# Cosine-similarity attention on one core: SyncE holds back the loads of the third pair until K of the first pair has landed

## The chip, the cores and the metric

The kernel runs on one core of a Trainium2 chip. Five engines work side by side, each through an instruction queue of its own, in order: TensorE (PE; its weight loads are listed as PEld), VectorE (DVE), ScalarE (ACT), GpSimd (POOL) and SyncE (SP), which here does nothing but issue transfers. ScalarE issues three transfers itself. The transfers are carried out by 16 DMA engines; SyncE and ScalarE each feed a queue of their own (q1 and q10 in the profile). An engine waits for another, or for a transfer, on a semaphore; a transfer has landed when its semaphore has counted 16, one from each DMA engine. The metric is the device time of one execution in microseconds, and smaller is better.

## The reference

For each of 8 batches and 12 heads, Q, K and V have 512 rows of 64 float32 numbers. Rows of Q and K are scaled to length 1, their scores are divided by tau = 0.1, and a softmax weights the rows of V:

```python
Q_norm = Q / (np.linalg.norm(Q, axis=-1, keepdims=True) + 1e-10)
K_norm = K / (np.linalg.norm(K, axis=-1, keepdims=True) + 1e-10)
scores = np.einsum('bhqd,bhkd->bhqk', Q_norm, K_norm) / tau
weights = np.exp(scores - np.max(scores, axis=-1, keepdims=True))
weights = weights / (np.sum(weights, axis=-1, keepdims=True) + 1e-10)
return np.einsum('bhqk,bhkd->bhqd', weights, V).astype(np.float32)
```

## The kernel before, in words

**Pairs.** Heads are worked on two at a time: 96 heads make 48 pairs, numbered from s = 0 in the code; the text counts from the first, so the third pair is s = 2. For a pair, Q, K and V are loaded in one transfer each of 256 KB (lines 310 to 314); a tile row of 128 partitions holds four rows of each head. The first pair is the exception: Q and K come in halves of one head, 128 KB each, Q on SyncE's queue and K on ScalarE's (lines 304 to 309).

**What happens to a pair.** Its Q and K are squared (in most pairs on GpSimd, L337; in the second pair on ScalarE with half of K on GpSimd, and in the third Q on ScalarE, L329, and K on GpSimd, L331). The squares are summed, partly on TensorE (L354) with a reduction on VectorE (L361). From the sums come the inverse lengths: for the first four pairs by a logarithm and an exponential on ScalarE (L248 and L252 for the first pair, L379 and L382 for the next three), later by steps on VectorE. Q and K are scaled with them (L258, L420), transposed on TensorE (L266, L268, L426) and copied back (L279, L434). TensorE then makes the scores, 512 x 512 a head, in four blocks (L508); ScalarE takes exp of each block, both heads in one instruction (L531; in the first pair's first two blocks one head at a time); TensorE multiplies with V (L548), which GpSimd has converted (L536); VectorE divides (L559, L561) and SyncE stores (L565).

**Order.** Operations are recorded with the operations that they need (`needs`), and each becomes one or several instructions. The order on each engine is a list written out by hand, `ORDER` (line 644), of the operations' numbers. `write` (line 69) turns an operation's needs into waits on semaphores just ahead of its instruction, so a wait stops everything behind it on that engine. SyncE's list begins

```python
"sp": (
    "7 8 64 65 103 104 11 141 142 66 179 180 105 222 223 143 ..."
```

which is: 7 and 8 the two halves of the first pair's Q; 64 and 65 Q and K of the second pair; 103 and 104 Q and K of the third; 11 V of the first; 141 and 142 Q and K of the fourth; 66 V of the second; 179 and 180 Q and K of the fifth; 105 V of the third; and so on. Stores come into the list after 33 loads. The halves of the first pair's K are 9 and 10, the first two entries of ScalarE's list.

ScalarE's list begins

```python
"act": (
    "9 10 3 12 25 16 18 17 29 31 67 30 68 106 44 74 75 40 41 45 112 47 113 ..."
```

where 3 loads the function table, 12 and 25 square the first pair's Q, 16 to 31 are the first pair's inverse lengths, 67 squares Q of the second pair, 30 is the last inverse length of the first pair, 68 squares half of K of the second pair, 106 squares Q of the third pair, and 44 is the first exponential of scores; 74 and 75 are the inverse lengths of the second pair, 112 and 113 those of the third.

**Buffers.** There are 15 buffers for Q and K of a pair and 10 for V (`RINGS`), so the first loads wait for no buffer: without the change, none of the transfers in the list's beginning waits for anything.

**Names.** `("LD", s, w)` is the load of Q (w = 0) or K (w = 1) of pair s, `("LD", 0, w, h)` that of head h of the first pair, `("LV", s)` that of V; `qk` is the buffer of Q and K, `sq` the squares, `qn` the scaled rows, `qt` the transposed ones, `scps` the scores, `et` their exponentials.

Of the kernel before, what the change touches and what calls it, by code (L numbers as in the profile page):

```python
# [108 lines left out]
def bass_cosine_similarity_attention_kernel(  # L109
# [15 lines left out]
    R_QK, R_V, R_SQ, R_QN, R_QT, R_ET, R_O, R_X = RINGS  # L125
# [31 lines left out]
    P = Program(nc)  # L157
# [15 lines left out]
    def src(x, s):  # L173
        b, h = divmod(2 * s, NHEAD)
        return x[b, h : h + 2].rearrange("h (p t) d -> p h (t d)", t=NT)

    def key(name, s, *rest):
        return (name, s) + rest if s >= 0 else None
# [111 lines left out]
    def squares(s, w):  # L290
        return [("SQ", s, w if s in SQ_ON else 0)] + ([("SQ", s, w, 1)] if s in SQ_ON and isinstance(SQ_ON[s][w], tuple) else [])
# [5 lines left out]
    def pair(s):  # L297
# [6 lines left out]
        for w, x in ((0, Q), (1, K)):  # L304
            if s == 0:
                for h in range(2):
                    P.add(("LD", 0, w, h), "act" if w else "sp", "ldh", -1000 + h,  [],
                          lambda e, w=w, x=x, h=h: e.dma_start(out=qk[iq][:, w, h], in_=src(x, s)[:, h]), slot=f"head{w}_{h}")  # L308
                continue
            P.add(("LD", s, w), "sp", "ld1" if s == 1 else "ld", s, [*([("SCL", 0, w, 0), ("SCL", 0, w, 1), ("SQ", 0, w, 0), ("SQ", 0, w, 1)] if s == R_QK else [key("SCL", s - R_QK, w), *(squares(s - R_QK, w) if s >= R_QK else [])])],  # L310
                  lambda e, w=w, x=x: e.dma_start(out=qk[iq][:, w], in_=src(x, s)),  # L311
                  slot=f"first{s}_{w}" if s <= 3 else f"qk{iq}")
        P.add(("LV", s), "sp", "ld", s + VLAG, [key("VC", s - R_V)],
# [32 lines left out]
        for w in range(2):  # L346
# [16 lines left out]
            else:  # L363
                P.add(("RED", s, w), "dve", "red", due_red(s) + 0.5 * w, [*sqs, ("NRMS", 0, 0, 1), *new(g - R_X), *last_direct(s)],
                      lambda e, w=w, dst=dst: e.tensor_reduce(  # L365
                          out=dst, in_=sq[iqs][:, 8 * w : 8 * w + 8, :], axis=AX.X, op=ALU.add))
# [47 lines left out]
        for w in range(2):  # L414
# [5 lines left out]
                  lambda e, w=w, r=r: e.tensor_tensor(  # L420
                      out=qn[iqn][:, w].rearrange("p t h d -> p h t d"),
                      in0=qk[iq][:, w].rearrange("p h (t d) -> p h t d", t=NT), in1=r, op=ALU.mult))
# [174 lines left out]
    for s in range(NP):  # L597
        pair(s)
# [171 lines left out]
```

## Time and profile before

| What | Value |
|---|---|
| time before, median of 3 runs (lowest, highest) | 189.58 us (189.12, 190.11) |
| the profiled execution's own time | 189.78 us |
| its span, first to last instruction | 187.8 us |
| ScalarE busy | 180.4 us, 96% of the span |
| TensorE busy | 173.9 us, 93% |
| VectorE busy | 173.0 us, 92% |
| GpSimd busy | 166.7 us, 89% |
| TensorE's clock, granted | 0.995 |
| bytes moved | 50.76 MB, 270 GB/s in the mean |

The groups of instructions that matter here (line, engine, operation, tiles, count; busy us, mean ns of one; idle time before them and what ended it):

```profile
L531 ACT ACTIVATE et<-scps 128x1024 bf16<-128x1024 f32 (+1 forms) x191 | 174.1, 1170 | 0.0
...
L331 POOL TENSOR_TENSOR sq<-qk 128x512 bf16<-128x512 f32 (+1 forms) x4 | 3.7, 932 | 2.0 <-DMA qk<-in_K_dram 2.0
```

ScalarE's exponentials alone take 174.1 us of the 187.8. Its other work and its idle time lie in the first 16 us and in the last two or three. The page's rows of transfers give, for each kind of issue, how long it took from issue to landing, in the median:

```profile
vf<-in_V_dram SPq DMA_DIRECT2D x48, 256.0 KB, 6.0
qk<-in_Q_dram SPq DMA_DIRECT2D x47, 256.0 KB, 5.3
qk<-in_K_dram SPq DMA_DIRECT2D x47, 256.0 KB, 6.1
...
qk<-in_Q_dram SPq DMA_DIRECT2D x2, 128.0 KB, 2.6
qk<-in_K_dram ACTq DMA_DIRECT2D x2, 128.0 KB, 2.8
```

and the rate over the span in 40 slices of 4.7 us, where the first three slices are the part of the kernel that the change touches:

```profile
DMA  5999999899999998999999799995987722311333
GB/s 162 326 355 350 348 354 330 258 316 320 380 384 379 349 332 250 336 276 337 378 382 366 220 285 379 362 328 162 317 294 226 244 85 71 112 58 62 110 108 121
```

An issue (DMA_DIRECT2D on SPq or ACTq) is the time in which the engine hands a transfer over; the transfer itself follows. On the timeline, rows of SPq are issues, not transfers.

### The profile page before, as it was taken

To read this page: it belongs to the slowest core of one execution; us is meant where nothing else is said; L and a number is where in the kernel's file an instruction comes from. 1 tells how busy PE (TensorE), PEld (TensorE's weight loads), DVE (VectorE), ACT (ScalarE), POOL (GpSimd) and SP (SyncE) were. 2 spreads that over 40 slices of the span, in tenths; PEclk is the share of its full clock that TensorE was granted. 3 is DMA by queue.
4 is the path that set the end of the run, shared out by engine and by line. 5 is a ranking of instruction groups with operands and counts; after the bars stand their busy time and mean duration, and the time that the engine had idled before them with its cause. 6 is when DMAs were issued, how large, how long until landed. Compare 5 with 4: busy or idle time off the path is not lost.

```text
span 187.8 us, 6632 instructions
## 1 busy us (share of the span) xinstructions
PE 173.9 (93%) x2694; PEld 108.4 (58%) x2694; DVE 173.0 (92%) x546; ACT 180.4 (96%) x212; POOL 166.7 (89%) x152
## 2 busy tenths in 40 slices
PE   6799899999998999999999999999999889999993
PEld 2455566566565666666566666556655556655562
DVE  2688999999999999999999999999999999998873
ACT  4699999999999999999999999999999999999992
POOL 5499999999999999999999999999999999965600
PEclk9999999999999999999999999999999999999998
DMA  5999999899999998999999799995987722311333
GB/s 162 326 355 350 348 354 330 258 316 320 380 384 379 349 332 250 336 276 337 378 382 366 220 285 379 362 328 162 317 294 226 244 85 71 112 58 62 110 108 121
DMA packets 52446, 50.76 MB, mean 270 GB/s; under 512 B 3136, under 2 KB 52416, under 8 KB 52416
## 3 DMA queue, kind: packets, MB, share of 16 engines
q1 hardware_dynamic: 51984, 50.02, 80.7%
q8 instruction: 21, 0.34, 0.8%
q10 hardware_dynamic: 432, 0.33, 0.5%
q14 instruction: 9, 0.07, 0.1%
HBM read 37.75 MB, written 12.58 MB: 268 GB/s over the span
## 4 chain that ended last, share of the span: by engine, by line
ACT 93%; DMA 3%; SPq 1%; issue 1%; PE 1%; DVE 1%
ACT et L531 92%; DMA qk<-in_Q_dram 3%; PE ops L576 1%; SPq L311 0%; SPq L308 0%; DVE ob L589 0%; ACT sq L329 0%; ACT ys L379 0%; ACT nps L382 0%; DVE rd L587 0%; PE tps L576 0%
## 5 line engine op out<-in xcount | busy, mean ns | idle before, releaser
L531 ACT ACTIVATE et<-scps 128x1024 bf16<-128x1024 f32 (+1 forms) x191 | 174.1, 1170 | 0.0
L337 POOL TENSOR_TENSOR sq<-qk 128x1024 bf16<-128x1024 f32 x44 | 82.7, 1893 | 0.5 <-DMA qk<-in_K_dram 0.5
L508 PE MATMUL scps<-qt 64*128 64x512 bf16 x380 | 75.2, 386 | 7.3 <-ACT et L531 3.5
L548 PE MATMUL ops<-vb,et 128*128 128x65 bf16 x1504 | 73.4, 194 | 0.1
L548 PEld LDWEIGHTS ops<-vb,et 128*128 128x128 bf16 x1504 | 55.7, 98 | 28.7 <-issue 21.1
L561 DVE TENSOR_TENSOR ob<-ops,rd 128x256 f32<-128x256 f32 x94 | 38.7, 418 | 0.4
L420 DVE TENSOR_TENSOR qn<-qk,nps 128x512 bf16<-128x512 f32 x58 | 38.6, 676 | 0.5 <-ACT nps L382 0.5
L420 POOL TENSOR_TENSOR qn<-qk,rk 128x512 bf16<-128x512 f32 x36 | 37.5, 1054 | 1.0 <-DVE rk L394 0.9
L426 PE MATMUL tps<-ident,qn 128*128 128x128 bf16 x376 | 33.9, 221 | 0.4 <-POOL qn L420 0.2
L434 DVE COPY qt<-tps 128x1024 bf16<-128x1024 bf16 x47 | 32.2, 684 | 1.3 <-PE tps L426 0.9
L508 PEld LDWEIGHTS scps<-qt 64*128 64x128 bf16 x380 | 18.8, 92 | 24.9 <-ACT et L531 11.7
L365 DVE TENSOR_REDUCE nps<-sq 128x8 f32<-128x512 bf16 x48 | 32.5, 681 | 0.0
L536 POOL TENSOR_SCALAR vb<-vf 128x512 bf16<-128x512 f32 x48 | 30.3, 646 | 0.2
L426 PEld LDWEIGHTS tps<-ident,qn 128*128 128x128 bf16 x376 | 21.5, 98 | 12.8 <-issue 6.0
L354 PE MATMUL ops<-sq,ident 128*128 128x64 bf16 x368 | 18.4, 193 | 0.8 <-ACT nps L252 0.8
L559 DVE RECIPROCAL rd<-ops 128x4 f32<-128x4 f32 x94 | 16.1, 175 | 2.9 <-PE ops L548 2.2
L354 PEld LDWEIGHTS ops<-sq,ident 128*128 128x128 bf16 x368 | 13.7, 98 | 3.9 <-issue 2.0
L361 DVE TENSOR_REDUCE nps<-ops 128x8 f32<-128x64 f32 x40 | 8.7, 217 | 0.6 <-PE ops L354 0.4
L480 POOL TENSOR_TENSOR xz<-xz 128x1024 f32<-128x1024 f32 x2 | 3.8, 1892 | 3.3 <-DVE xz L475 3.3
L389 DVE TENSOR_TENSOR nps<-nps,ys 128x32 f32<-128x32 f32 (+1 forms) x30 | 6.2, 208 | 0.2
L390 DVE SCALAR_TENSOR_TENSOR nps<-nps,ys 128x32 f32<-128x32 f32 (+1 forms) x30 | 6.2, 208 | 0.0
L331 POOL TENSOR_TENSOR sq<-qk 128x512 bf16<-128x512 f32 (+1 forms) x4 | 3.7, 932 | 2.0 <-DMA qk<-in_K_dram 2.0
(61 smaller groups left out, 64.2 us busy)
## 6 DMA issues: line engine op xcount, KB each, us to landing
vf<-in_V_dram SPq DMA_DIRECT2D x48, 256.0 KB, 6.0
qk<-in_Q_dram SPq DMA_DIRECT2D x47, 256.0 KB, 5.3
qk<-in_K_dram SPq DMA_DIRECT2D x47, 256.0 KB, 6.1
out_dram<-ob SPq DMA_DIRECT2D x47, 256.0 KB, 4.2
qk<-in_Q_dram SPq DMA_DIRECT2D x2, 128.0 KB, 2.6
qk<-in_K_dram ACTq DMA_DIRECT2D x2, 128.0 KB, 2.8
out_dram<-ob SPq DMA_DIRECT2D x1, 128.0 KB, 1.7
out_dram<-ob ACTq DMA_DIRECT2D x1, 64.0 KB, 1.6
```

What stands on the lines that cost most here:

```text
L337: lambda e: e.tensor_tensor(out=sqf, in0=data, in1=data, op=ALU.mult))
L354: last = e.matmul(out=o_ps[bank][:, 320:384], lhsT=ident[:, :], rhs=sq[iqs][:, 8 * w : 8 * w + 8, 8 * k : 8 * k + 8], start=(k == 0), stop ...
L365: lambda e, w=w, dst=dst: e.tensor_reduce(out=dst, in_=sq[iqs][:, 8 * w : 8 * w + 8, :], axis=AX.X, op=ALU.add))
L420: lambda e, w=w, r=r: e.tensor_tensor(out=qn[iqn][:, w].rearrange("p t h d -> p h t d"), in0=qk[iq][:, w].rearrange("p h (t d) -> p h t d" ...
L426: last = e.transpose(t_ps[:, w, t, :], qn[iqn][:, w, t].rearrange("p h d -> p (h d)"), ident[:, :])
L434: lambda e: e.tensor_copy(out=qt[iqt][:, :, :, :].rearrange("p w t x -> p (w t x)"), in_=t_ps[:, :, :, :].rearrange("p w t x -> p (w t x)")))
L508: last = e.matmul(out=sc_ps[:, 2 * b + h, :], lhsT=qt[iqt][64 * h : 64 * h + 64, 1, c, :], rhs=qt[iqt][64 * h : 64 * h + 64, 0, :, :], sta ...
L531: lambda e, c=c, b=b, hs=hs: e.activation(out=et[iet][:, c, hs[0] : hs[-1] + 1, :], in_=sc_ps[:, 2 * b + hs[0] : 2 * b + hs[-1] + 1, :], f ...
L536: lambda e: e.tensor_scalar(out=vb[:, iq, :, :, 0:DIM].rearrange("p c h d -> p h c d"), in0=vf[iv][:, :, :].rearrange("p h (c d) -> p h c ...
L548: last = e.matmul(out=o_ps[h][:, 65 * t : 65 * t + 65], lhsT=et[iet][:, c, h, 128 * t : 128 * t + 128], rhs=vb[:, iq, c, h, :], start=(c = ...
L559: lambda e, h=h, grid=grid: e.reciprocal(out=rd[io][:, h, :], in_=grid[:, :, DIM]))
L561: lambda e, h=h, grid=grid: e.tensor_tensor(out=ob[io][:, h], in0=grid[:, :, 0:DIM], in1=rd[io][:, h, :].unsqueeze(2).to_broadcast([128, N ...
```

## The change

The load of Q of the third pair, `("LD", 2, 0)`, gets one more need: `("LD", 0, 1, 1)`, the load of K of the first pair's second head. SyncE thus waits on that load's semaphore (16 counts) before it issues operation 103, and all that stands behind 103 in its list waits with it. The lists of all engines are unchanged, and so are all other needs.

```diff
-            P.add(("LD", s, w), "sp", "ld1" if s == 1 else "ld", s, [*([("SCL", 0, w, 0), ("SCL", 0, w, 1), ("SQ", 0, w, 0), ("SQ", 0, w, 1)] if s == R_QK else [key("SCL", s - R_QK, w), *(squares(s - R_QK, w) if s >= R_QK else [])])],
+            P.add(("LD", s, w), "sp", "ld1" if s == 1 else "ld", s, [*([("LD", 0, 1, 1)] if (s, w) == (2, 0) else []), *([("SCL", 0, w, 0), ("SCL", 0, w, 1), ("SQ", 0, w, 0), ("SQ", 0, w, 1)] if s == R_QK else [key("SCL", s - R_QK, w), *(squares(s - R_QK, w) if s >= R_QK else [])])],
                   lambda e, w=w, x=x: e.dma_start(out=qk[iq][:, w], in_=src(x, s)),
                   slot=f"first{s}_{w}" if s <= 3 else f"qk{iq}")
```

## The prediction

> **What bounds the kernel now.** I began with the page's chain of work that ended last, then had the same chain in order of time, and then the timelines of ScalarE and SyncE over the first 16 us.
>
> ```profile
> ## 4 chain that ended last, share of the span: by engine, by line
> ACT 93%; DMA 3%; SPq 1%; issue 1%; PE 1%; DVE 1%
> ```
>
> ```profile
> 2.67 5.60 DMA qk<-in_Q_dram
> 8.27 0.02 issue
> 8.29 0.63 ACT sq L329
> 8.92 0.48 ACT et L531
> ...
> 15.53 167.90 ACT et L531 x183
> ```
>
> The reader is to see two regimes. From 8.29 us on, ScalarE works without a gap to 183.43 us, so the end follows from when that run begins. What releases its beginning is a transfer: Q of the third pair, issued at 2.67 us and landed 5.60 us later, and that is the first load that the change holds back. ScalarE's own lines say where it stood still before:
>
> ```profile
> 5.64 0.20 ACT L252 ACTIVATE xs<-ys 128x4 f32<-128x4 f32 x1
> 6.85 0.63 ACT L329 ACTIVATE sq<-qk 128x512 bf16<-128x512 f32 x1 [1.01 <-DMA qk<-in_Q_dram]
> 7.39 0.16 ACT L252 ACTIVATE nps<-ys 128x4 f32<-128x4 f32 x1
> 7.61 0.42 ACT L329 ACTIVATE sq<-qk 128x256 bf16<-128x256 f32 x1
> 8.29 0.63 ACT L329 ACTIVATE sq<-qk 128x512 bf16<-128x512 f32 x1 [0.27 <-DMA qk<-in_Q_dram]
> 8.83 0.58 ACT L531 ACTIVATE et<-scps 128x512 bf16<-128x512 f32 x1
> ```
>
> Each row is start, duration, instruction and, in brackets, the idle time before it. It waits 1.01 us for Q of the second pair and 0.27 us for Q of the third; its queue is in order, so the first exponential (L531) stands behind both squares. A later landing of the third pair's Q therefore moves the end one for one, and an earlier one can return at most these 1.28 us.
>
> **The change, part by part.** It adds one wait in SyncE's queue and nothing else: no instruction, transfer or position in any queue changes. SyncE comes to the gated load at 2.67:
>
> ```profile
> 2.16 0.47 SPq L311 DMA_DIRECT2D qk<-in_K_dram  x1
> 2.67 0.47 SPq L311 DMA_DIRECT2D qk<-in_Q_dram  x1
> 3.18 0.47 SPq L311 DMA_DIRECT2D qk<-in_K_dram  x1
> 3.70 0.47 SPq L314 DMA_DIRECT2D vf<-in_V_dram  x1
> 4.21 0.56 SPq L311 DMA_DIRECT2D qk<-in_Q_dram  x1
> ```
>
> *When the gate opens.* K of the first pair goes out on ScalarE's queue in two halves, the two issues together 0.79 to 1.68 us. For the second the issue view says 2.9 us to landing, and GpSimd, which squares both halves in 0.612 us each without a gap from 3.56, takes it at 4.17. So the gate opens at about 4.15 and the third pair's Q is issued at 4.2 instead of 2.67: 1.5 us later. Behind it, in SyncE's order, stand K of the third pair, V of the first, Q and K of the fourth, V of the second and so on; all move by 1.5 us at first.
>
> *What hides it.* A load issued into this queue is not short of time, it stands in line. The third pair's Q took 5.6 us to land in the trace, but SyncE's queue at 33.44 us, nearly drained, shows the same 256 KB load without a line before it:
>
> ```profile
> 33.44 0.47 SPq L311 DMA_DIRECT2D qk<-in_Q_dram  x1
> ...
> DMA to landing us min/median/max: 2.8/2.8/2.8
> ```
>
> So 4.2 + 2.8 = 7.0 us is the earliest landing after the change. The line before it is unchanged: K of the second pair is issued at 2.16 as before and lands 5.4 us later, at 7.6; from there on the loads landed 0.7 us apart (issue plus landing: 7.6, 8.3, 9.0, 9.8, 10.5, 11.3, 12.0). Whoever is queued by the time its predecessor ends lands one step behind it: 7.6 + 0.7 = 8.3, as before. Cost of the gate on this load: 0. If the cover goes, because the second pair lands sooner, the bound is 7.0, which is 1.3 us before the 8.27 of the trace; so the K that opens the gate could land 1.2 us later than it did and still cost nothing.
>
> *The loads behind it.* The same restart gives their landings when the line is short: 36.2, 37.0, 38.1, 39.1, 39.8, 41.1 and 41.8, that is 0.93 us apart in the mean against 0.74 in the long line. Put on 4.2 us that is 7.0, 7.7, 8.8, 9.9, 10.6 and 11.9, each before the 8.3, 9.0, 9.8, 10.5, 11.3 and 12.0 of now. The bound from the bad side takes both: the old 8.3 for the first and 0.93 for each step, which gives 9.2, 10.1, 11.0, 11.9, so 0.2 us late for K of the third pair up to 0.6 for K of the fourth. Their slack:
>
> ```profile
> 9.10 1.04 POOL L331 TENSOR_TENSOR sq<-qk 128x512 bf16<-128x512 f32 x1 [0.84 <-DMA qk<-in_K_dram]
> ...
> 10.68 0.23 DVE L361 TENSOR_REDUCE xs<-ops 128x8 f32<-128x64 f32 x1
> ...
> 11.19 0.32 ACT L379 ACTIVATE ys<-xs,eps 128x16 f32<-128x16 f32 x1
> ```
>
> K of the third pair goes through GpSimd's square, TensorE and a reduction that ends at 10.91, and ScalarE's logarithm wants it at 11.19: 0.28 us of slack, so 0.2 is free. K of the fourth is squared as the second of two that GpSimd does from 10.81 (2.04 us together), so it is wanted at about 11.83 and would come 0.1 late; the logarithm at 14.20 has its input at 14.14. That makes 0 to 0.1 us on ScalarE. I take 0, the nearer side, since the line is still there when the gate opens. SyncE itself catches up: it issues in 0.5 us steps what the transfers take 0.7 for, and from 10.65 us on the old queue held it back at about 0.7 per issue anyway.
>
> *What could be gained.* The gate keeps SyncE quiet from 2.63 to 4.2 us. The stretches there (PE, weight loads, DVE, ACT, POOL, clock, DMA share, GB/s) show that transfers were slow just then:
>
> ```profile
> 3.20:4.20 1.00, 1.00 (x4) 0.37 (x3) 0.42 (x1) 0.61 (x2) 0.61 (x1) 1.00 0.92 243
> 4.20:5.20 1.00, 1.00 (x5) 0.45 (x4) 1.00 (x3) 0.73 (x4) 0.61 (x1) 1.00 0.69 210
> ```
>
> From 2.0 to 3.2 us it was 321 GB/s. If the issuing behind them caused the dip, it cost (321 - 243) + (321 - 210) = 189 KB, or 0.59 us of landing for the second pair. Bounds: 0 to 0.59, and 1.28 if all of ScalarE's waiting went. I take 0, because the same slowness (267 to 312 GB/s a microsecond from 34 to 39 us) stands at the other place where the line is short, with SyncE issuing at the same 0.47 us pace as here; a gate makes the line shorter, not longer.
>
> Does the gate speed K itself? In the stretch 2.0 to 4.2 us the issue view gives 0.37 MB to SyncE's queue and 0.26 MB to ScalarE's, so the two do share; but K's halves land 2.7 and 2.9 us after issue and Q's 2.5 and 2.8. Bound: 0.2 us at most.
>
> The Trainium skill, DMA: Bandwidth & Descriptors, section on queues, rings and completion order, has each engine consume one row's descriptors in ring order and take turns between rows. By that rule the third pair's packets stand behind the second pair's on SyncE's row, and holding them back frees nothing for K or for the second pair: the sum would be 0 and the faster rival falls. By the row of the dip alone it would be up to -0.59 us. The trace agrees in that SyncE's loads land in the order of issue.
>
> **Sum.** Gate on the third pair's Q 0, loads behind it 0 (to +0.1), gain for the second pair 0 (to -0.59): 0.0. Against the profiled execution that is 189.78 us (span 187.8 and 2.0 around it), which lies 0.2 above the median of the runs shown, 189.58. On the median I forecast 189.6, with the forecast's own range 189.1 to 190.1, the spread of those runs.
>
> **The rivals.**
>
> *Slower: the line is not what sets the landing.* If issue to landing stays at 5.6 us for the third pair's Q (every load from 1.69 to 4.81 us took 5.1 to 6.5), it lands at 4.2 + 5.6 = 9.8, ScalarE waits 1.5 us more at the square L329 and every exponential behind it moves: 191.1. It decides from the point where that landing passes 8.27. Against it: the 2.8 us at 33.44, and 3.0 and 3.6 for the two behind. For it: the second pair's line may hide a slow stretch of transfers that comes with any restart, and the third pair would now meet it, in the one place with no slack. Chance 0.27.
>
> *Faster: the issuing caused the dip.* Then the second pair's Q lands 0.59 to 1.0 us sooner and the wait before L329 shrinks; TensorE's sums, the head's second half and the first exponential follow. 0.6 to 1.28 us off: 188.3 to 189.0, middle 188.6. For it: the dip's place, right behind four issues without a pause. Against it: the dip at 34 to 39 us. Chance 0.22.
>
> *The gate does nothing*, K having landed by the time SyncE comes: excluded by 1.5 us in this execution; it would be 189.6. Chance 0.02; forecast 0.49.
>
> **How the numbers follow.** Half a per cent (0.95 us) is about what a measurement of this kernel can tell from no change. Forecast and idle gate lie within it (0.51), the slower rival beyond it (0.27), the faster around its edge and counted beyond it (0.22). The range reaches to both: from 188.5, which leaves out only the full 1.28, to 191.1.
>
> **What would show it.** In the changed trace SyncE's third pair goes out at 4.2; right, if its landing takes about 4.1 us instead of 5.6 and ScalarE's square of it still starts near 8.3, with the exponentials gapless behind. The slower rival shows as a wait well over 0.27 us there, the faster as a wait under 1.01 before the second pair's square and over 243 and 210 GB/s in the two stretches. A gap in ScalarE after 11 us would refute the slack of the loads behind; a first pair's K that lands after 5.4 us would refute the gate's time.

## The result, and the profile after

| | Before | After |
|---|---|---|
| median of 22 runs each | 189.28 us | 189.84 us |
| lowest, highest | 188.90, 190.11 | 189.22, 190.90 |
| the profiled execution's own time, its span | 189.78, 187.8 us | 189.81, 187.9 us |

The ratio after to before is 1.0034, with a 95% interval of 1.0018 to 1.005: 0.34% slower, some 0.6 us, inside the half per cent that the prediction called no change, but clear of 1. It is the only set of runs of the changed kernel: the experiments below were timed in three later sets on three chips, each beside runs of the kernel before, and in these the changed kernel ran only singly.

Part of the difference is in a few executions. In five of the 22 changed runs TensorE's granted clock was 0.991 over the span; these are the five slowest, 190.57 to 190.90 us. The other 17, at 0.995 and above, have a median of 189.81, so the median does not hang on them. Of the kernel before, no run that the comparisons in three other sets use, 64 in all, is under 0.995.

The two profiled executions differ by 0.1 us of span only: the one of before had a late beginning among its kind, as further traces show below. What the change does can be read from them all the same. First the chain of waits of the changed kernel in order of time (start, length, what):

```profile
1.23 3.16 DMA qk<-in_K_dram
4.38 0.02 issue
4.40 3.98 DMA qk<-in_Q_dram
8.38 0.02 issue
8.40 0.63 ACT sq L329
...
15.65 167.89 ACT et L531 x183
```

The chain now begins with K of the first pair on ScalarE's queue, which lands at 4.38 and opens the gate; the third pair's Q is issued at 4.40 and lands 3.98 us later at 8.38, where it took 5.60 us from 2.67 to 8.27 before. The same end, by another way. ScalarE's timeline in the changed kernel (start, length, instruction, idle time before it):

```profile
5.88 0.20 ACT L252 ACTIVATE xs<-ys 128x4 f32<-128x4 f32 x1
6.00 0.61 ACT L329 ACTIVATE sq<-qk 128x512 bf16<-128x512 f32 x1
6.52 0.16 ACT L252 ACTIVATE nps<-ys 128x4 f32<-128x4 f32 x1
6.61 0.40 ACT L329 ACTIVATE sq<-qk 128x256 bf16<-128x256 f32 x1
8.40 0.63 ACT L329 ACTIVATE sq<-qk 128x512 bf16<-128x512 f32 x1 [1.39 <-DMA qk<-in_Q_dram]
8.94 0.58 ACT L531 ACTIVATE et<-scps 128x512 bf16<-128x512 f32 x1
```

The wait of 1.01 us for the second pair's Q is gone: the data landed at 5.88, 0.95 us sooner than in the first trace of the kernel before. All of it went into the wait for the third pair's Q, 1.39 us in place of 0.27. A gain and a new wait of nearly the same size, behind each other on one in-order queue. The stretches (PE, weight loads, DVE, ACT, POOL, clock, DMA share, GB/s) show both sides on the DMA engines:

```profile
3.20:4.20 1.00, 1.00 (x4) 0.36 (x3) 0.42 (x1) 0.51 (x2) 0.61 (x1) 1.00 0.77 240
4.20:5.20 1.00, 1.00 (x4) 0.44 (x3) 0.86 (x3) 0.81 (x4) 0.61 (x1) 1.00 0.84 282
5.20:6.20 1.00, 0.88 (x8) 0.39 (x6) 0.64 (x2) 0.69 (x5) 0.65 (x2) 1.00 0.64 196
```

From 4.2 to 5.2 us the transfers run at 282 GB/s instead of 210, while the second pair comes in; from 5.2 to 6.2 they fall to 196, where before it was 299. Further traces bear both out: 282 to 336 GB/s in the first of these stretches in three traces of the changed kernel against 210 to 262 in four of the kernel before, and 196 to 237 in the second against 299 to 345. That reads as a line running dry while what SyncE issued at 4.40 is not flowing yet; it is worked out from the rates, and the counts below support it.

### The profile page after: what moved, and what is told of

It is laid out like the page before. It is cut to its first block, busy times and chain, and to the rows that moved or that the text cites. A ratio compares the mean times of both kernels' runs of the same rounds, so it can differ in the third digit from the quotient of the medians.

```text
span 187.9 us, 6632 instructions
## 1 busy us (share of the span) xinstructions
PE 174.4 (93%) x2694; PEld 108.7 (58%) x2694; DVE 172.9 (92%) x546; ACT 180.3 (96%) x212; POOL 166.8 (89%) x152
## 4 chain that ended last, share of the span: by engine, by line
ACT 93%; DMA 4%; PE 1%; issue 1%; DVE 1%; ACTq 0%
ACT et L531 92%; DMA qk<-in_Q_dram 2%; DMA qk<-in_K_dram 2%; PE ops L576 1%; DVE ob L589 0%; ACT sq L329 0%; ACT ys L379 0%; ACT nps L382 0%; ACTq L308 0%; DVE rd L587 0%; PE tps L576 0%
```

## The experiments

One table holds the reading of all traces, so that single landings are not made too much of; the recorded expectations call a profiled execution a look. "Lands" is the time at which the load's semaphore has its sixteenth count in the trace; "step" is how long the third pair's Q lands behind the second pair's K; "exp" is the start of the first exponential of scores.

| Trace | third pair's Q issued | second pair's Q lands | second pair's K | third pair's Q | step | exp | span |
|---|---|---|---|---|---|---|---|
| before | 2.67 | 6.83 | 7.58 | 8.27 | 0.69 | 8.83 | 187.8 |
| before, e5 | 2.67 | 6.15 | 6.86 | 7.53 | 0.67 | 8.09 | 187.1 |
| before, e6 | 2.67 | 6.75 | 7.43 | 8.17 | 0.74 | 8.73 | 187.7 |
| before, e11 | 2.68 | 6.50 | 7.25 | 7.98 | 0.73 | 8.54 | 187.5 |
| changed | 4.40 | 5.88 | 6.52 | 8.38 | 1.86 | 8.94 | 187.9 |
| changed, e7 | 4.17 | 5.57 | 6.25 | 7.66 | 1.41 | 8.22 | 187.3 |
| changed, e12 | 4.05 | 5.51 | 6.18 | 7.86 | 1.68 | 8.42 | 187.4 |
| changed, exp first, e4 | 4.07 | 5.51 | 6.19 | 8.22 | 2.03 | 8.04 | 187.6 |
| gate earlier, e9 | 3.37 | 5.51 | 6.14 | 8.03 | 1.89 | 8.59 | 187.6 |
| gate later, e3 | 6.03 | 6.01 | 6.69 | 8.73 | 2.04 | 9.29 | 189.3 |
| gate one load down, e2 | 2.67 | 6.11 | 6.79 | 7.48 | 0.69 | 8.04 | 187.1 |
| gate two down, e1 | 2.67 | 5.44 | 6.43 | 7.15 | 0.72 | 7.71 | 186.9 |
| gate two down, later, e10 | 2.67 | 6.15 | 6.88 | 7.55 | 0.67 | 8.11 | 187.6 |
| before, exp first, e8 | 2.67 | 5.29 | 6.49 | 7.16 | 0.67 | 8.07 | 187.6 |

In every trace in which the third pair's Q goes out ungated, it lands 0.67 to 0.74 us behind the second pair's K (8 of 8); in every one in which a gate stands ahead of it, 1.41 to 2.04 us behind (6 of 6). And in all traces of the kernel before and of the changed one the span is 179.0 to 179.1 us more than the start of the first exponential, of which the last 4.4 us lie behind the last exponential.

A load lands with the last of its sixteen counts, one from each DMA engine, and the traces hold each count. They show that the longer step has two parts. The eighth count of the third pair's Q comes 1.12 to 1.42 us behind the eighth of the second pair's K in the changed kernel (e4 included), against 0.68 to 0.89 in the eight ungated traces: the whole load is late. On top of that a few engines lag in some traces: in e4 fifteen counts are in at 7.05 and the sixteenth at 8.22. In e9 the eighth count is only 0.94 behind and fifteen are in at 7.24, but the sixteenth comes at 8.03. The second pair's Q has such stragglers too: eight of its counts are in at 4.64 to 5.09 us in all fourteen traces, and the last few counts spread its landing from 5.29 to 6.83.

### Gate two loads down (e1)

V of the first pair and all behind it wait; Q and K of the third pair do not.

```diff
-        P.add(("LV", s), "sp", "ld", s + VLAG, [key("VC", s - R_V)],
+        P.add(("LV", s), "sp", "ld", s + VLAG, [key("VC", s - R_V), *([("LD", 0, 1, 1)] if s == 0 else [])],
```

> The gate is moved two loads down: Q and K of the third pair go out as before the change (2.67 and 3.18 us), and V of the first pair and all behind it wait for K of the first pair's second head. Theory T (trade): the change has two effects that cancel: with SyncE quiet, Q of the second pair lands about 0.9 us sooner (5.9 against 6.8), and Q of the third pair, issued late, lands no sooner than before (8.4). Then here, with fewer issues behind the second pair than before the change, Q of the second pair lands at 6.0 to 6.5, Q of the third at 7.0 to 7.7, ScalarE's wait ahead of the third pair's square stays under 0.5 us, and the time is 0.4 to 0.9 us below the kernel before (ratio 0.995 to 0.998). Rival S (scatter): the second pair's sooner landing in the changed kernel's trace was chance; then Q of the second pair lands at 6.5 to 7.0, Q of the third at 8.0 to 8.4, and the time is that of before within 0.3 us.

Measured: 189.12 us against 189.18, ratio 0.9998 (0.9979 to 1.0017). ScalarE in its trace:

```profile
5.72 0.61 ACT L329 ACTIVATE sq<-qk 128x512 bf16<-128x512 f32 x1
...
7.17 0.63 ACT L329 ACTIVATE sq<-qk 128x512 bf16<-128x512 f32 x1 [0.30 <-DMA qk<-in_Q_dram]
7.71 0.58 ACT L531 ACTIVATE et<-scps 128x512 bf16<-128x512 f32 x1
```

Both waits are short and the exponentials begin 1.1 us before those of the first trace of the kernel before, as theory T said, with the second pair's Q even sooner (5.44) than its 6.0 to 6.5; but the median does not follow (theory S). The profiled execution, at 188.90 us, was below its own median. So no cost shows once the third pair's Q and K are ahead of the gate; a gain does not show.

### Gate one load down (e2)

```diff
-[*([("LD", 0, 1, 1)] if (s, w) == (2, 0) else []), ...
+[*([("LD", 0, 1, 1)] if (s, w) == (2, 1) else []), ...
```

> The gate is moved one load down: Q of the third pair goes out at 2.67 us as before the change, K of the third pair and all behind it wait for K of the first pair's second head. Theory T: Q of the second pair lands at 5.9 to 6.3, Q of the third right behind the second pair's K, at 6.8 to 7.4, so ScalarE's two waits both shrink; K of the third pair is issued at 4.4 and lands at 8.2 to 8.6, no later than before (9.03). Time 0.5 to 1.2 us below the kernel before (ratio 0.994 to 0.997). Rival S: second pair's Q at 6.5 to 7.0, third pair's Q at 8.0 to 8.4; K of the third pair comes late; the time is 0 to 0.5 us above the kernel before.

Measured: 189.28 us against 189.18, ratio 0.9997 (0.9979 to 1.0014). Only the third pair's Q has been taken out of the gate, everything behind it is still held (its K is issued at 4.26), and no cost shows: this interval ends below the one in which the changed kernel's ratio lies (1.0018 to 1.005). So the median's cost hangs on this one load being behind the gate, as far as different sets can be compared; the changed kernel was not run beside e1 and e2. K of the third pair, held by over a microsecond, lands at 8.15 all the same, sooner than in any trace of the kernel before (8.25 to 9.03). The gain that theory T wanted did not come here either.

### Gate later (e3)

```diff
-[*([("LD", 0, 1, 1)] if (s, w) == (2, 0) else []), ...
+[*([("LD", 1, 0)] if (s, w) == (2, 0) else []), ...
```

> The gate waits for Q of the second pair instead of K of the first: it opens at about 5.9 us, 1.5 us later than in the change. If the third pair's Q sets the start of the gapless run and its landing follows its own issue (theory T, 4.0 us from issue to landing in the changed kernel), it lands at 9.3 to 9.9, ScalarE waits 1.0 to 1.5 us longer ahead of its square, and the time is 1.5 to 2.0 us above the kernel before (ratio 1.008 to 1.011). If its landing is set by the line before it, as predicted (rival L), or by 2.8 us from issue on an empty line, it lands at 8.3 to 8.7 and the time stays within 0.3 us of the changed kernel (ratio 1.002 to 1.005).

Measured: 191.16 us against 189.18, ratio 1.0105 (1.0066 to 1.0144). The time is theory T's, but the landing is the rival's: the third pair's Q landed 2.7 us after its issue, at 8.73, where T had 9.3 to 9.9 and 2.8 us on an empty line gives 8.3 to 8.7. So T met the time by luck. The gate is so late that the line is empty, and the stretches of this kernel show what a restart costs when nothing hides it (columns as above):

```profile
6.50:7.00 0.50, 0.47 (x10) 0.28 (x10) 0.50 (x3) 0.50 (x3) 0.34 (x2) 1.00 0.00 0
7.00:7.25 0.25, 0.25 (x10) 0.23 (x6) 0.25 (x2) 0.13 (x1) 0.25 (x1) 1.00 0.58 98
7.25:7.50 0.25, 0.25 (x4) 0.09 (x1) 0.22 (x2) 0.00 (x0) 0.12 (x1) 1.00 0.72 119
7.50:8.00 0.50, 0.50 (x11) 0.34 (x11) 0.47 (x2) 0.00 (x0) 0.00 (x0) 1.00 0.92 307
```

Issued at 6.03, the load moves no byte until 7.0 and the rate is 307 GB/s from 7.5. The first exponential is 0.35 us later than in the changed kernel's first trace, and the span 1.4 us longer. The rest came behind. ScalarE's timeline shows two gaps, both ended by scores from TensorE:

```profile
14.10 1.02 ACT L531 ACTIVATE et<-scps 128x1024 bf16<-128x1024 f32 x1 [0.17 <-PE scps L508]
15.61 1.02 ACT L531 ACTIVATE et<-scps 128x1024 bf16<-128x1024 f32 x1 [0.29 <-PE scps L508]
```

TensorE's granted clock (the third number from the end) fell to half just there. These are the same stretch of e3 and of the changed kernel:

```profile
12.17:15.58 3.41, 3.37 (x31) 1.63 (x29) 2.27 (x5) 2.98 (x5) 2.67 (x4) 0.50 1.05 351
```

```profile
12.17:15.58 3.41, 3.25 (x52) 2.01 (x50) 2.78 (x6) 3.41 (x8) 3.12 (x3) 1.00 1.09 362
```

TensorE was busy all through it in e3, with 31 matmuls instead of 52, and a pair of score matmuls took 0.61 us instead of 0.39. That explains the gaps of this one execution. It does not explain the set: four of its six runs have a clock of 0.995 to 0.998 and still take 190.67 to 191.23 us. What delays those was not traced; in e10 below, loads that come late make such a gap at full clock. The changed kernel's trace has no gap between 10 and 42 us.

### The changed kernel with the first exponential ahead of the square (e4), and the same exchange before the change (e8)

```diff
-"9 10 3 12 25 16 18 17 29 31 67 30 68 106 44 74 75 ..."
+"9 10 3 12 25 16 18 17 29 31 67 30 68 44 106 74 75 ..."
```

> The changed kernel with one exchange in ScalarE's list: the first exponential of scores stands ahead of the third pair's square instead of behind it. If ScalarE's in-order wait for the third pair's Q is what the change costs (theory T), 0.4 to 0.6 us of that wait (1.39 us) is filled with the exponential, and the time falls by 0.4 to 0.6 us from the changed kernel, to about that of the kernel before (ratio 0.999 to 1.001). If the cost lies elsewhere, in K of the third pair or the loads behind (rival B), TensorE's sums of the third pair and the logarithm stay late, and the time stays at that of the changed kernel (ratio 1.003 to 1.004).

Measured: 189.54 us against 189.18, ratio 1.0017 (0.9998 to 1.0036), between theory T's range and rival B's.

> The kernel before with the first exponential ahead of the third pair's square in ScalarE's list. If the third pair's Q sets the start of the gapless run in most executions of the kernel before too, and not in its first look alone, then up to half of the exponential (0.3 us) fills the wait: ratio 0.998 to 0.9995. If it does not, the scores on TensorE do, and the exchange gives nothing or costs up to 0.3 us (ratio 0.9995 to 1.0015): then the changed kernel's gain from the same exchange (0.3 us) is the wait that the gate made.

Measured: 189.67 us against 189.09, ratio 1.0031 (1.0012 to 1.0049). The kernel before loses by the exchange, about twice what was allowed for. ScalarE's timelines in e8 (two lines) and in e4 (one) show what the exchanged exponential waits for:

```profile
4.59 0.42 ACT L239 ACTIVATE sq<-qk 128x256 bf16<-128x256 f32 x1 [1.08 <-DMA qk<-in_Q_dram]
...
8.07 0.60 ACT L531 ACTIVATE et<-scps 128x512 bf16<-128x512 f32 x1 [0.70 <-PE scps L508]
```

```profile
8.04 0.60 ACT L531 ACTIVATE et<-scps 128x512 bf16<-128x512 f32 x1 [1.36 <-PE scps L508]
```

The scores come from TensorE at 8.0 us in both, and now the square stands behind that wait. In e8 a square whose data landed at 7.16 is held up; in e4 the square's data are not there at 8.04 (8.22), so the exponential fills the wait. But e8's trace is not typical: the second halves of the first pair landed at 4.57 and 4.74, against 3.83 to 4.14 (Q) and 4.09 to 4.32 (K) in the four traces of the kernel before, which delays the scores. In those four the scores are ready 0.23 to 0.34 us after the third pair's Q has landed, so there too the exchange would make ScalarE wait longer. The exchange costs 0.31% without the gate; with it the measured ratio is 1.0017 where the changed kernel's own was 1.0034. These two intervals overlap widely and come from different sets, so this is weak support, not proof, that ScalarE's in-order wait carries the cost.

### Further traces (e5, e6, e11 of the kernel before; e7, e12 of the changed one)

No edit; their readings stand in the table. Each is one execution.

> The kernel before, once more, for a second look at its first 9 us. Theory S (scatter): the 6.83 us at which the second pair's Q landed in the first look was late by chance; landings vary from one execution to the next, and here it lands at 5.4 to 6.9 and the third pair's Q at 7.1 to 8.3, with the start of the first exponential 0.55 us behind that, and a span of 179.0 us more than this start (187.8 less 8.83 in the first look). Theory T (issuing behind them slows them): the second pair's Q at 6.6 to 7.0 and the third pair's at 8.1 to 8.4 again, in each look.

> The kernel before, a third look. Theory S: as in the second look, second pair's Q anywhere from 5.4 to 6.9, third pair's Q 7.1 to 8.3; the middle of the three looks lies under 6.5 and 7.9. Theory T: 6.6 to 7.0 and 8.1 to 8.4.

> The changed kernel, a second look. Under both theories the second pair's Q lands at 5.4 to 6.2. The third pair's Q, issued at 4.1 to 4.4 when its gate opens, lands 3.7 to 4.2 us later, at 8.0 to 8.5, if the restart after the quiet stretch sets it (theory R); if its landing follows the second pair's K by 0.7 us, as the prediction had it (theory L), at 6.9 to 7.4.

> The kernel before, a fourth look, for the spread of the second pair's landing without a gate (6.83, 6.15 and 6.75 so far; with a gate 5.4 to 6.1 in six looks). Theory T: 6.1 to 6.9 again. Theory S: it may come under 6.0. Third pair's Q 1.4 us behind it in both, and the span 179.0 us more than the start of the first exponential.

> The changed kernel, a third look. Second pair's Q at 5.5 to 5.9; third pair's Q 3.4 to 4.2 us after its issue and 1.4 to 2.0 us behind the second pair's K, at 7.6 to 8.4; ScalarE's wait ahead of its square 0.9 to 1.4 us; the span 179.0 us more than the start of the first exponential.

The kernel before landed its second pair's Q at 6.15 to 6.83 in four traces, the changed one at 5.51 to 5.88 in three: the gap that theory T asks for, with a scatter that theory S asks for. Neither met its numbers in full: e5's 6.15 is outside T's 6.6 to 7.0, and the middle of the first three, 6.75, is not under S's 6.5. Among the ungated kernels e8 is against T (5.29), though there the first pair came late, and e10 below, quiet from 3.65 us, shows 6.15. That quiet behind the second pair speeds it is likely, not shown.

The third pair's Q of e7 landed at 7.66, between theory R's 8.0 to 8.5 and theory L's 6.9 to 7.4; its step of 1.41 us, and 1.68 in e12, is against L's 0.7. ScalarE's wait ahead of the square in e7 and in e12:

```profile
7.68 0.63 ACT L329 ACTIVATE sq<-qk 128x512 bf16<-128x512 f32 x1 [0.91 <-DMA qk<-in_Q_dram]
```

```profile
7.88 0.63 ACT L329 ACTIVATE sq<-qk 128x512 bf16<-128x512 f32 x1 [1.22 <-DMA qk<-in_Q_dram]
```

One more thing has to be said of these traces. On average the first exponential starts at 8.55 us in the four of the kernel before and at 8.53 in the three of the changed one: they do not contain the 0.6 us. The median span of the timed runs does: 187.85 us for the changed kernel, and 187.1, 187.2 and 187.4 for the kernel before in the three other sets. With 179.0 us behind it that puts the typical first exponential at about 8.85 against 8.1 to 8.4, which is worked out and was not seen. The two single executions e7 and e12 were timed at 188.99 and 189.39 where the kernel before had medians of 189.09 and 189.28 on the same chips, so the cost does not show in these two.

### Gate earlier (e9)

```diff
-[*([("LD", 0, 1, 1)] if (s, w) == (2, 0) else []), ...
+[*([("LD", 0, 1, 0)] if (s, w) == (2, 0) else []), ...
```

> The gate waits for K of the first pair's first head instead of the second: it opens at about 3.5 us, 0.7 us before the changed kernel's. If the changed kernel's cost is that the line runs dry (theory R: its second pair is through the fastest DMA engines at 5.1 us and the data of the gated load flow 1.5 us after its issue), a gate at 3.5 has the load in the line by 5.0: the third pair's Q lands 0.7 to 1.0 us behind the second pair's K, at 6.9 to 7.6, no dip in the stretch 5.2 to 6.2 us, and the time is that of the kernel before (ratio 0.999 to 1.001). If any gate in SyncE's queue costs by the time it holds (rival P, in proportion: 0.6 us for 1.5 us of holding), half of the cost stays: ratio 1.0015 to 1.002.

Measured: 189.29 us against 189.28, ratio 1.0007 (0.9985 to 1.0029). The time is theory R's, and there is no dip from 5.2 to 6.2 us (324 GB/s). The landing in the trace misses: the third pair's Q landed at 8.03, 1.89 us behind the second pair's K, not 0.7 to 1.0, with the slow stretch now from 6.2 to 7.2 (264 GB/s). But that is one count: fifteen of the sixteen were in at 7.24, inside theory R's 6.9 to 7.6, and the eighth came 0.94 us behind the second pair's. In the same trace one count of the second half of the first pair's Q was as late (fifteen at 3.91, the last at 4.69). So by rate and counts the line did not run dry here, and the long step is one DMA engine that delivered late; whether the gate has a part in that is open. The interval does not exclude rival P's 1.0015 to 1.002.

### Gate two loads down and later (e10)

```diff
-        P.add(("LV", s), "sp", "ld", s + VLAG, [key("VC", s - R_V)],
+        P.add(("LV", s), "sp", "ld", s + VLAG, [key("VC", s - R_V), *([("LD", 1, 0)] if s == 0 else [])],
```

> The gate stands ahead of V of the first pair, as in the first experiment, but opens only when Q of the second pair has landed (5.4 to 6.1 us), so that SyncE is quiet from 3.65 us until then. Theory T (issuing behind the second pair slows it): second pair's Q at 5.3 to 5.7, third pair's Q at 6.7 to 7.1, first exponential at 7.3 to 7.7. Theory S (scatter): second pair's Q at 5.4 to 6.8, third pair's Q 1.4 us behind it. In both the loads behind come about 1.7 us later than in the kernel before; if that shows, as it did with the later gate in the third experiment, it is as a second gap of ScalarE after 15 us, and the time is 0 to 0.8 us above the kernel before; without it 0 to 0.6 us below.

Measured: 189.54 us against 189.28, ratio 1.0019 (0.9993 to 1.0046). Theory T's landing for the second pair's Q (5.3 to 5.7) missed with 6.15; theory S's, and its 1.4 us from there to the third pair's Q, held. The first exponential starts early (8.11), but a second gap follows. These are lines of GpSimd, TensorE and ScalarE in this kernel:

```profile
16.19 1.90 POOL L337 TENSOR_TENSOR sq<-qk 128x1024 bf16<-128x1024 f32 x1 [0.34 <-DMA qk<-in_K_dram]
```

```profile
18.14 0.41 PE L354 MATMUL ops<-sq,ident 128*128 128x64 bf16 x8 [0.71 <-POOL sq L337]
```

```profile
18.91 23.94 ACT L531 ACTIVATE et<-scps 128x1024 bf16<-128x1024 f32 x26 [0.41 <-PE scps L508]
```

GpSimd's square waits for K, TensorE's sums wait for the square, and the scores behind them come late. V and the loads behind it were held for 0.4 us in e1 and for one microsecond in e2 without a gap; held for 2.5 they make one. None of the variants beats the kernel before beyond its interval.

## Why the prediction was right, and where it was not

- **The time.** Forecast 189.6 with no change, its own range 189.1 to 190.1; measured 189.84, 0.34% above before. That it stays within half a per cent was right, and the sum of 0.0 was off by about 0.6 us. That 189.6 lies within 0.3 us of 189.84 is in part luck: the forecast started from the median of three runs, 189.58, and the median of 22 is 189.28.
- **The term that was mis-sized** is "Gate on the third pair's Q 0", and in it the sentence that whoever is queued by the time its predecessor ends lands one step of 0.7 us behind it. The step was 1.41 to 2.04 us in all six traces with a gate ahead of that load. Taken as 1.7 it puts the load 1.0 us later behind the second pair's K than the prediction had it. The 2.8 us from issue to landing on an empty line was right where the line was empty (2.7 in e3), and not for a load that comes into a line about to run dry: 3.5 to 4.0 us in the changed kernel, 4.7 with the earlier gate. Even there eight of the sixteen counts were in 2.5 to 2.7 us after the issue in the changed kernel; the landing waits for the last one.
- **The gain** that was set at 0 came in the second pair's landing: 5.5 to 5.9 us against 6.2 to 6.8. It is about as large as the added step, so the two nearly cancel at the third pair's Q: 7.66 to 8.38 us against 7.53 to 8.27. The forecast's landing near 8.3 was right in the first trace by two errors of opposite sign, which is luck.
- **The rivals.** Both mechanisms are in the trace. The slower rival's sign, "a wait well over 0.27 us there", is met with 1.39, 0.91 and 1.22; the faster rival's, a second pair's square without its wait and a faster stretch from 4.2 to 5.2 us, too. Neither got its price: in the traces the one takes up the other.
- **The chip's queues.** From the ring order that the Trainium skill, DMA: Bandwidth & Descriptors, section on queues, rings and completion order, states, the prediction concluded that holding back what stands behind frees nothing for the loads ahead. The loads of the second and third pair landed in the order of issue in every trace. Further on the prediction's sentence that SyncE's loads land in the order of issue does not hold: in the kernel before the Q issued at 6.35 landed at 11.90, ahead of the V issued at 5.79, which landed at 12.02. The conclusion does not look safe either, as the second pair came sooner in the changed kernel's three traces than in the four of before.
- **When the gate opens**: forecast 4.15, measured 4.03 to 4.38. **The loads behind**: forecast to be free, and they are within what was measured: e2 holds all of them and no cost shows, and no second gap shows in the changed kernel's three traces. The five runs at a clock of 0.991 were not traced.
- **What stays open**: why single DMA engines deliver late and whether the gate makes that more frequent, how much of the second pair's sooner landing is the gate's doing, why the clock fell in five of the changed runs, and why single traces of the two kernels average alike when their medians differ by 0.56 us. The cause of that difference is located by e1 and e2, not seen in a trace.

## What to carry to other kernels

A wait put ahead of a load can cost more than issue-to-landing times suggest: here the load behind the gate landed 1.4 to 2.0 us behind its predecessor instead of 0.7. So gate only loads that no in-order engine is about to wait for: with the same gate one load down (e2) no cost showed. And where the end hangs on a scattered start, take several traces, and a set of runs of both kernels side by side, before giving a difference of half a microsecond to a cause.

## What was not expected of the hardware

With the line empty, a load on SyncE's queue moved its first byte 1.0 us after its issue began, and the rate reached 307 GB/s after 1.5 us (e3: issue at 6.03, 0 GB/s until 7.0, 307 GB/s from 7.5). The same 256 KB load of the second pair, issued at 1.68 to 1.70 us in every trace, landed anywhere from 5.29 to 6.83 us, and that scatter alone spans 1.5 us of the kernel's beginning; half of its sixteen counts were in by 5.09 in all of them. And a stretch of 3.41 us at half of TensorE's clock, while TensorE was busy (e3, 12.17 to 15.58), shows over the whole span only as a granted clock of 0.991.
